# Down-weight sums of a two-FFN encoder layer, queued pair by pair behind a store of the gate and up stage

## The chip, the cores and the metric

One core of a Trainium2 chip runs the whole layer as one program. The metric is the device time of one execution, in microseconds; lower is better. Engines are named as the profile does: PE (TensorE matmuls), PEld (its weight loads), DVE (VectorE), ACT (ScalarE), POOL (GpSimd), SP (SyncE, which here issues most loads).

## The reference

One layer of a hybrid encoder on x of shape (1, 1024, 1024) in float32: an FFN, a mixing sub-layer (attention and a two-way recurrent scan) and a second FFN, each between RMS norms. The change touches the FFNs alone:

```python
def _swiglu(h, w_gate, w_up, w_down):
    return (jax.nn.silu(h @ w_gate) * (h @ w_up)) @ w_down

f = _swiglu(_rmsnorm(h, ffn1_pre_g), ffn1_w_gate, ffn1_w_up, ffn1_w_down)
h = h + 0.5 * _rmsnorm(f, ffn1_post_g)
# ... mixing sub-layer ...
f = _swiglu(_rmsnorm(h, ffn2_pre_g), ffn2_w_gate, ffn2_w_up, ffn2_w_down)
h = h + 0.5 * _rmsnorm(f, ffn2_post_g)
```

w_gate and w_up are 1024 x 2816, w_down is 2816 x 1024.

## The kernel before

Every float32 product is made of three passes: an operand is split into a rounded high part and the rest (`halves`, `split`: ACT makes the high part on L185, DVE the rest on L186), and PE adds high x high, high x low and low x high.

Both matrix products of an FFN are made by a fast scheme of seven products of half-size blocks in place of eight. In the **gate and up stage** the two matrices are the two block rows; one step j treats a column of 128 features. There are 22 columns. For each j, four weight blocks raw (two of the gate, two of the up weights, 256 KB each) are loaded by SP (L283) into a ring of eight buffers, DVE combines them (`left`, L60 to L63; L60 is the first and reads both up blocks), seven products of 12 matmuls run on PE (`multiply`, L81, numbered 1, 2, 6, 7, 5, 3, 4 in that order) into PSUM tiles gu, and DVE and ACT gather them (`gather`, L86 and after). A split weight is in a ring of eight (wh, wl).

When product 3 or 4 of a column has been gathered, `store` multiplies the two results on DVE (L114) and keeps a tile. Two columns make a *pair* m; its four tiles are the blocks of the left operand of the **down stage**. From them POOL forms the differences and sums that the seven down products need (L117, L126) and stores all seven to DRAM (`put`, L116, tensor d_hid). The tile that ends the pair's first column is called a11; its call of `store` sends it off with `put(1, ...)`, and then a21 minus it with `put(7, ...)`.

The right operand of the down stage also needs sums of blocks, here of w_down, which depend on no activation. `down_sums(m)` makes them: SP loads four blocks of w_down (L181 by way of `load`) into four tiles ws0 to ws3, POOL makes four differences in place (L145) and stores each to DRAM (L146, tensor d_ws). Each of the four tags has one buffer, so a pair's loads must wait until the stores of the pair before have left it. The down stage reads d_ws first in its third product.

The order on each engine is not written by hand. A scheduler takes the traced instructions, with the data and buffer dependences between them, and lists them per engine by priority and readiness; every engine and every DMA queue then works through its list in order. An instruction that depends on nothing but weights may so be listed far ahead of where the code writes it.

Of the kernel before, what the change touches and what calls it, by code (L numbers as in the profile page):

```python
# [36 lines left out]
class _GateUp:  # L37
# [72 lines left out]
    def store(self, j, half, x):  # L110


        G, H = self.K.nc.gpsimd, self.H
        self.K.nc.vector.tensor_tensor(x[:, 0], x[:, 0], x[:, 1], op=OP.mult)  # L114
        H[j % 2, half] = x
        put = lambda n, y: G.dma_start(self.hid[n - 1, j // 2], y)  # L116
        sub = lambda o, a, b: G.tensor_tensor(o, a, b, op=OP.subtract)  # L117
        if (j % 2, half) == (0, 0):
            a11, a21 = H[0, 0], H[0, 1]
            put(1, a11[:, 0])  # L120
            sub(a21[:, 1], a11[:, 0], a21[:, 0])
            put(7, a21[:, 1])
        elif (j % 2, half) == (1, 1):
            a11, a21, a22 = H[0, 0], H[0, 1], H[1, 1]
            put(4, a22[:, 0])
            G.tensor_tensor(a22[:, 1], a21[:, 0], a22[:, 0], op=OP.add)  # L126
            put(5, a22[:, 1])
            sub(a11[:, 1], a22[:, 1], a11[:, 0])
            put(6, a11[:, 1])
        elif (j % 2, half) == (1, 0):  # L130
            a11, a12 = H[0, 0], H[1, 0]
            put(2, a12[:, 0])
            sub(a12[:, 1], a12[:, 0], a11[:, 1])
            put(3, a12[:, 1])
            H.clear()
# [16 lines left out]
    def rest(self, f, psum):  # L152
        for j in range(NJ):
            for n in (1, 2, 6, 7, 5, 3, 4):
                if (n, j) not in self.done:
                    self.multiply(n, j, f, psum)
                if (n, j) in self.P:
                    self.gather(n, j)
            if j % 2 == 0:
                self.down_sums(j // 2)  # L160


class _Kernel:
# [84 lines left out]
    def post(self, p, ft, t, gb, scale, res, store):  # L248

        nc = self.nc  # L250
        rows = slice(t * 128, (t + 1) * 128)
        r = p.tile([128, D], F32, name="res", tag="res")
        self.load(r, res[rows, :])
        rs = self.inv_rms(p, ft, scale)
        nc.vector.scalar_tensor_tensor(ft, ft, rs, gb, op0=OP.mult, op1=OP.mult)  # L255
        nc.vector.tensor_tensor(ft, ft, r, op=OP.add)  # L256
        self.nc.sync.dma_start(store[rows, :], ft)
# [9 lines left out]
    def hand_over(self, p, psum, f, i, order, gb, scale, res, store, gcol, x, ready=lambda half: None):  # L267

        self.post(p, f[order[i]], order[i], gb, scale, res, store)
        for j in ([i - 1] if i % 4 else []) + ([i] if i % 4 == 3 else []):  # L270
            if i == j == NT - 1:
                ready(0)
            self.pre(p, f[order[j]])
            if j % 4 == 3:
                self.feature_major(psum, [f[t] for t in order[j - 3:j + 1]], gcol, x, 0, j // 4)
        if i == NT - 1:
            ready(1)
# [1155 lines left out]
```

## Time and profile before

| | |
|---|---|
| median of 3 runs | 2482.37 us (2478.59 to 2485.76) |
| profiled execution | 2491.72 us, span 2489.9 us |
| PE busy | 2255.0 us (91%) |
| DVE busy | 1708.7 us (69%) |
| ACT busy | 1041.1 us (42%) |
| POOL busy | 575.1 us (23%) |
| mean granted PE clock | 0.933 |
| L145, sums of down weights on POOL | 88, 118.2 us |
| ws loads, d_ws stores | 88 and 88, 256.0 KB each |

The first FFN's gate and up stage runs from the start to about 510 us of the span, the second's from about 1800 to 2260 us. Busy times overlap between engines. A row such as "A <- B: t, n, x" in the views of waits says that A's engine stood idle for t us in n pieces, the longest of x us, and that B ended that. Numbers are microseconds from the span's start; a view of windows gives the busy time of each engine in each stretch.

### The profile page before, as it was taken

The page shows a single profiled execution, that of the slowest core. Times are in us where ns is not written, and L with a number is a line of the kernel's source. Part 1 is how long each engine was busy: PE and PEld are TensorE (multiplying, and loading weights), DVE is VectorE, ACT ScalarE, POOL GpSimd, SP SyncE. Part 2 cuts the span into 40 slices and gives each one's busy share as a digit, 9 for nine tenths or more (in the row PEclk, how much of TensorE's full clock was granted, in tenths as well). Part 3 has the DMA queues.
Part 4 walks back from the last instruction along what each step waited for, and adds up shares of the span by engine and source line. Part 5 has one row for each costly group of instructions (what it writes and reads, how often), then busy time and mean ns, then how long its engine had stood idle before and what let it go on. Part 6 is the DMA issues. An engine that isn't in the chain of part 4 may idle for free. (4 is left out here: it accounts for less than half of the span.)

```text
span 2489.9 us, 39287 instructions
## 1 busy us (share of the span) xinstructions
PE 2255.0 (91%) x14532; PEld 1818.7 (73%) x14532; DVE 1708.7 (69%) x2917; ACT 1041.1 (42%) x1918; POOL 575.1 (23%) x668
## 2 busy tenths in 40 slices
PE   5869999999999998999987698888778899999997
PEld 4657888878877676778766576765556788887886
DVE  8768877765676345666566767725896987876565
ACT  4313333354577403656445354444431233335452
POOL 7772221210000010111101211122368422221000
PEclk8889999999999998999996688888889899999999
DMA  5773333376662414322366766467567433336655
GB/s 149 232 228 110 110 106 98 110 242 193 196 223 93 185 43 151 85 76 72 99 172 170 174 160 171 118 198 234 169 204 252 156 107 102 105 107 234 195 188 182
DMA packets 359763, 386.03 MB, mean 155 GB/s; under 512 B 73618, under 2 KB 268050, under 8 KB 359572
## 3 DMA queue, kind: packets, MB, share of 16 engines
q1 hardware_dynamic: 314272, 289.02, 38.6%
q0 software_dynamic: 27248, 86.05, 9.4%
q10 hardware_dynamic: 18052, 8.46, 1.3%
q8 instruction: 114, 1.87, 0.3%
q14 instruction: 77, 0.63, 0.1%
HBM read 257.53 MB, written 125.89 MB: 154 GB/s over the span
## 5 line engine op out<-in xcount | busy, mean ns | idle before, releaser
L81 PE MATMUL gu<-xh,wh 128*128 128x512 f32 x704 | 282.1, 401 | 47.3 <-DVE row L86 44.1
L185 ACT ACTIVATE wh<-raw 128x512 fp32r<-128x512 f32 (+1 forms) x273 | 169.5, 630 | 367.9 <-PE gu L81 261.1
L86 DVE TENSOR_TENSOR row<-gu,row 128x512 f32<-128x512 f32 x308 | 207.0, 684 | 122.8 <-PE gu L81 122.1
L81 PE MATMUL gu<-xl,wh 128*128 128x512 f32 x704 | 279.5, 397 | 0.0
L81 PE MATMUL gu<-xh,wl 128*128 128x512 f32 x704 | 278.8, 396 | 0.6 <-DVE wl L186 0.6
L186 DVE TENSOR_TENSOR wl<-raw,wh 128x512 fp32r<-128x512 f32 (+1 forms) x273 | 260.1, 955 | 4.8 <-ACT wh L185 4.1
L414 PE MATMUL pd<-gl,gwh 128*128 128x512 f32 x616 | 240.4, 390 | 2.5 <-DVE gl L186 2.5
L414 PE MATMUL pd<-gh,gwh 128*128 128x512 f32 x616 | 239.5, 390 | 0.6 <-DVE row L86 0.6
L414 PE MATMUL pd<-gh,gwl 128*128 128x512 f32 x616 | 239.7, 389 | 0.0
L186 DVE TENSOR_TENSOR gwl<-graw,gwh 128x512 fp32r<-128x512 f32 (+1 forms) x176 | 110.5, 631 | 129.4 <-ACT gwh L185 127.5
L116 POOL DMA_DIRECT2D d_hid<-row x154 | 84.7, 551 | 489.6 <-DVE row L114 470.3
L81 PEld LDWEIGHTS gu<-xh,wh 128*128 128x128 f32 x704 | 136.1, 193 | 78.8 <-DVE row L86 46.4
L185 ACT ACTIVATE gwh<-graw 128x512 fp32r<-128x512 f32 (+1 forms) x176 | 101.4, 576 | 193.4 <-PE pd L414 162.2
L81 PEld LDWEIGHTS gu<-xh,wl 128*128 128x128 f32 x704 | 135.2, 192 | 29.3 <-DVE wl L186 0.8
L81 PEld LDWEIGHTS gu<-xl,wh 128*128 128x128 f32 x704 | 135.7, 193 | 28.3
L414 PEld LDWEIGHTS pd<-gl,gwh 128*128 128x128 f32 x616 | 115.6, 188 | 27.8 <-DVE gl L186 4.2
L414 PEld LDWEIGHTS pd<-gh,gwh 128*128 128x128 f32 x616 | 115.6, 188 | 25.3 <-DVE row L86 1.0
L414 PEld LDWEIGHTS pd<-gh,gwl 128*128 128x128 f32 x616 | 115.7, 188 | 24.0
L145 POOL TENSOR_TENSOR ws<-ws 128x512 f32<-128x512 f32 x88 | 118.2, 1343 | 46.6 <-DMA ws<-in_ffn_w_down_dram 45.6
L186 DVE TENSOR_TENSOR gl<-raw,gh 128x512 fp32r<-128x512 f32 x160 | 112.2, 713 | 16.4 <-ACT gh L185 16.0
L185 ACT ACTIVATE gh<-raw 128x512 fp32r<-128x512 f32 x160 | 98.0, 620 | 29.2 <-DMA raw<-in_ffn_w_down_dram 20.1
L114 DVE TENSOR_TENSOR row<-row 128x512 f32<-128x512 f32 x88 | 95.7, 1089 | 3.7
(354 smaller groups left out, 5248.1 us busy)
## 6 DMA issues: line engine op xcount, KB each, us to landing
d_hid<-row POOLq DMA_DIRECT2D x154, 256.0 KB, 2.5
graw<-d_hid SPq DMA_DIRECT2D x132, 256.0 KB, 3.1
raw<-in_ffn_w_gate_dram SPq DMA_DIRECT2D x88, 256.0 KB, 3.1
raw<-in_ffn_w_up_dram SPq DMA_DIRECT2D x88, 256.0 KB, 2.9
ws<-in_ffn_w_down_dram SPq DMA_DIRECT2D x88, 256.0 KB, 3.5
d_ws<-ws POOLq DMA_DIRECT2D x88, 256.0 KB, 2.8
raw<-d_ws SPq DMA_DIRECT2D x88, 256.0 KB, 2.7
raw<-in_ffn_w_down_dram SPq DMA_DIRECT2D x66, 256.0 KB, 3.3
```

What stands on the lines that cost most here:

```text
L81: self.K.nc.tensor.matmul(ps, a[:, k, :], b[:, k, :], start=(k == 0 and i == 0), stop=(k == 3 and i == 2))
L86: add = lambda o, x: V.tensor_tensor(o, ps, x, op=OP.add)
L114: self.K.nc.vector.tensor_tensor(x[:, 0], x[:, 0], x[:, 1], op=OP.mult)
L116: put = lambda n, y: G.dma_start(self.hid[n - 1, j // 2], y)
L145: G.tensor_tensor(o, a, b, op=OP.subtract)
L185: self.nc.scalar.activation(h, src, AF.Copy)
L186: (eng or self.nc.vector).tensor_tensor(l, src, h, op=OP.subtract)
L414: T.matmul(ps[x], a[:, ts], b, start=(m == 0 and k == 0), stop=(m == NM - 1 and k == 2))
```

## The change

`down_sums` is traced in a block that gives every POOL instruction in it (the four differences and the four stores) an edge to `begun`, the POOL instruction that stores the pair's own a11. The edge fixes the order of issue on POOL alone; nothing waits for that store to end. The loads of ws on SP get no edge of their own; the scheduler places them anew, since the buffers they fill come free at other times.

```diff
@@ store
         if (j % 2, half) == (0, 0):
             a11, a21 = H[0, 0], H[0, 1]
-            put(1, a11[:, 0])
+            self.begun = put(1, a11[:, 0])
             sub(a21[:, 1], a11[:, 0], a21[:, 0])
             put(7, a21[:, 1])
@@ rest
             if j % 2 == 0:
-                self.down_sums(j // 2)
+                with self.K.tc.issue_after(self.begun.ins):
+                    self.down_sums(j // 2)
```

The changed file is one line longer, so lines from L160 on count one higher in it.

On POOL, first FFN, the place of the first stores of gate and up tiles (d_hid0). Tiles carry numbers here: row_613 is a11 of pair 0, row_612 and row_617 are its a21 and a22, and ws_2284 to ws_2287 are the down-weight tiles of pair 5. Before:

```order
L145 TENSOR_TENSOR ws_2285<-ws_2287,ws_2285 128x512
L146 DMA d_ws0_92<-ws_2285 128x512
L145 TENSOR_TENSOR ws_2287<-ws_2287,ws_2284 128x512
L146 DMA d_ws0_92<-ws_2287 128x512
L116 DMA d_hid0_86<-row_613 128x512
L117 TENSOR_TENSOR row_612<-row_613,row_612 128x512
L116 DMA d_hid0_86<-row_617 128x512
L116 DMA d_hid0_86<-row_612 128x512
L126 TENSOR_TENSOR row_617<-row_612,row_617 128x512
L116 DMA d_hid0_86<-row_618 128x512
L116 DMA d_hid0_86<-row_617 128x512
L117 TENSOR_TENSOR row_613<-row_617,row_613 128x512
```

Ahead of these rows stand the 20 sums of pairs 0 to 4 and the first of pair 5. Now (ws_794 to ws_797 are those of pair 0):

```order
L342 TENSOR_TENSOR row_220<-row_220,row_224 128x512
L343 TENSOR_TENSOR row_224<-row_224,row_220 128x512
L116 DMA d_hid0_86<-row_617 128x512
L116 DMA d_hid0_86<-row_613 128x512
L117 TENSOR_TENSOR row_612<-row_613,row_612 128x512
L145 TENSOR_TENSOR ws_794<-ws_795,ws_794 128x512
L116 DMA d_hid0_86<-row_612 128x512
L146 DMA d_ws0_92<-ws_794 128x512
L145 TENSOR_TENSOR ws_795<-ws_797,ws_795 128x512
L126 TENSOR_TENSOR row_617<-row_612,row_617 128x512
L146 DMA d_ws0_92<-ws_795 128x512
L145 TENSOR_TENSOR ws_797<-ws_797,ws_794 128x512
```

The sums of pair 0 now come behind the store of row_613 and between the other stores of that pair, and no sum of another pair is ahead of them; each later pair's four stand in the same way behind its own a11.

On SP, first FFN, the loads of the weights of block column 4 (gate: raw_1178 and raw_1200, up: raw_1221 and raw_1223), among loads of down weights. Before (ws_1965 to ws_1968 belong to pair 4, ws_2284 to ws_2287 to pair 5, ws_2603 and ws_2604 to pair 6):

```order
L181 DMA ws_1965<-in_ffn1_w_down_dram 128x512
L181 DMA ws_1966<-in_ffn1_w_down_dram 128x512
L181 DMA ws_1968<-in_ffn1_w_down_dram 128x512
L181 DMA ws_1967<-in_ffn1_w_down_dram 128x512
L181 DMA ws_2284<-in_ffn1_w_down_dram 128x512
L181 DMA ws_2285<-in_ffn1_w_down_dram 128x512
L181 DMA ws_2287<-in_ffn1_w_down_dram 128x512
L181 DMA ws_2286<-in_ffn1_w_down_dram 128x512
L283 DMA raw_1221<-in_ffn1_w_up_dram 128x4x128
L181 DMA ws_2603<-in_ffn1_w_down_dram 128x512
L181 DMA ws_2604<-in_ffn1_w_down_dram 128x512
L283 DMA raw_1223<-in_ffn1_w_up_dram 128x4x128
```

Now (raw_1067 and raw_1069 are up blocks of column 3, raw_1343 to raw_1386 blocks of column 5, ws_1008 to ws_1011 belong to pair 1):

```order
L284 DMA raw_1067<-in_ffn1_w_up_dram 128x4x128
L284 DMA raw_1069<-in_ffn1_w_up_dram 128x4x128
L284 DMA raw_1178<-in_ffn1_w_gate_dram 128x4x128
L284 DMA raw_1200<-in_ffn1_w_gate_dram 128x4x128
L284 DMA raw_1221<-in_ffn1_w_up_dram 128x4x128
L284 DMA raw_1223<-in_ffn1_w_up_dram 128x4x128
L182 DMA ws_1008<-in_ffn1_w_down_dram 128x512
L182 DMA ws_1009<-in_ffn1_w_down_dram 128x512
L284 DMA raw_1343<-in_ffn1_w_gate_dram 128x4x128
L182 DMA ws_1011<-in_ffn1_w_down_dram 128x512
L284 DMA raw_1365<-in_ffn1_w_gate_dram 128x4x128
L182 DMA ws_1010<-in_ffn1_w_down_dram 128x512
```

Before, 22 ws loads of pairs 1 to 6 and the four of pair 0 stand ahead of the last up block of column 4 (raw_1223). Now only pair 0's four do, and pair 1's come after it. The second FFN changes in the same way, and there the last pair's four ws loads and sums stand where the down stage's first loads begin, as in the first.

## The prediction

> **What bounds the kernel now.** I read the page first, then the stages by windows, then what each engine waited for in the two that were not full, and last the order of the two queues there.
>
> ```profile
> span 2489.9 us, 39287 instructions
> PE gu L81 13%; PE pd L414 8%; POOL ws L145 1%; PE po L1063 1%; DMA ws<-in_ffn_w_down_dram 1%; DMA raw<-in_ffn_w_up_dram 1%; DMA f_y<-d_y 1%; DVE wl L186 1%; DMA d_ws<-ws 1%; DVE row L255 0%; DVE row L256 0%; DMA d_y<-yb 0%; PE st L936 0%; PE var L1003 0%; DVE row L265 0%
> L86 DVE TENSOR_TENSOR row<-gu,row 128x512 f32<-128x512 f32 x308 | 207.0, 684 | 122.8 <-PE gu L81 122.1
> L186 DVE TENSOR_TENSOR wl<-raw,wh 128x512 fp32r<-128x512 f32 (+1 forms) x273 | 260.1, 955 | 4.8 <-ACT wh L185 4.1
> d_ws<-ws POOLq DMA_DIRECT2D x88, 256.0 KB, 2.8
> ```
>
> PE's gate and up matmuls are the largest piece of the chain that ended last (13%), and the sums' own line (ws L145) and their DMAs stand on that chain with 1% each, which is odd for work that nothing needs before the down stage. The next view takes four stretches of the two gate and up stages; its columns are the window, its length, busy time (with count) of PE, PEld, DVE, ACT and POOL, the granted clock, the DMA share and GB/s.
>
> ```profile
> 100.00:200.00 100.00, 74.18 (x304) 60.00 (x303) 74.38 (x73) 20.01 (x36) 70.85 (x80) 0.86 0.65 215
> 225.00:500.00 275.00, 275.00 (x1215) 227.72 (x1214) 216.32 (x287) 88.37 (x145) 64.11 (x79) 1.00 0.32 103
> 1850.00:1950.00 100.00, 80.72 (x337) 64.98 (x336) 76.66 (x80) 21.87 (x39) 75.51 (x83) 0.90 0.69 233
> 1950.00:1975.00 25.00, 25.00 (x112) 20.68 (x111) 24.88 (x28) 7.17 (x13) 11.88 (x15) 1.00 0.39 141
> ```
>
> From 225 to 500 us PE is busy all the time at clock 1.00: 1215 rows in 275 us, 0.2263 us a matmul. That is the pace of the stage. From 100 to 200 us the same stage passes only 304 rows at a mean clock of 0.86, and in the second FFN 337 rows in 100 us at 0.90. The time is lost early in each FFN, not spread over it. The gaps of PE there (start, length, instruction, idle time before it and its releaser):
>
> ```profile
> 129.10 0.79 PE L81 MATMUL gu<-xh,wh 128*128 128x512 f32 x1 [6.11 <-DVE row L86]
> 152.38 0.50 PE L81 MATMUL gu<-xh,wh 128*128 128x512 f32 x1 [1.82 <-DVE row L86]
> 189.61 0.80 PE L81 MATMUL gu<-xh,wh 128*128 128x512 f32 x1 [17.89 <-DVE row L86]
> ...
> 1901.45 0.54 PE L81 MATMUL gu<-xh,wh 128*128 128x512 f32 x1 [2.66 <-DVE row L86]
> 1937.99 0.79 PE L81 MATMUL gu<-xh,wh 128*128 128x512 f32 x1 [15.61 <-DVE row L86]
> ```
>
> 25.8 us of gaps in the first FFN, 18.3 us in the second, all ended by the DVE addition that empties a bank of gu (L86). DVE itself was starved, not busy. Its waits in the two FFNs, then SyncE's queue between 60 and 200 us (columns: us in total, times, longest):
>
> ```profile
> DVE s L60 <- DMA raw<-in_ffn_w_up_dram: 26.0, 4, 14.8
> DVE s L60 <- DMA raw<-in_ffn_w_up_dram: 24.0, 5, 13.4
> SPq L181 <- DMA d_ws<-ws: 65.0, 31, 5.6
> SPq L181 <- POOL ws L145: 22.7, 9, 5.4
> ```
>
> DVE's in-order queue stood for 26.0 and 24.0 us behind the first addition of a block column's combinations (L60), which wants two blocks of the up weights. SyncE's queue, which issues those loads in order, stood for 65.0 + 22.7 us behind loads of down weights (L181) whose tile ws was not yet free. The longest wait, row by row:
>
> ```profile
> 160.04 0.38 SPq L283 DMA_DIRECT2D raw<-in_ffn_w_gate_dram  x1
> 164.44 6.88 SPq L181 DMA_DIRECT2D ws<-in_ffn_w_down_dram  x3
> 171.41 0.39 SPq L283 DMA_DIRECT2D raw<-in_ffn_w_up_dram  x1
> 171.89 3.88 SPq L181 DMA_DIRECT2D ws<-in_ffn_w_down_dram  x2
> 175.85 0.40 SPq L283 DMA_DIRECT2D raw<-in_ffn_w_up_dram  x1
> 180.61 1.71 DVE L60 TENSOR_TENSOR s<-raw 128x512 f32<-128x512 f32 x1 [14.81 <-DMA raw<-in_ffn_w_up_dram]
> ```
>
> The two up loads went out at 171.41 and 175.85, each behind ws loads, and DVE, idle for 14.81 us, could go on only at 180.61; PE stood until 189.61. The chain that ended last says the same of the second FFN (start, length, what):
>
> ```profile
> 1919.66 3.98 DMA d_ws<-ws
> 1924.43 4.23 DMA raw<-in_ffn_w_up_dram
> 1930.64 2.39 DVE wl L186
> ```
>
> A store of one sum, then the up load that stood behind the next ws load, then DVE. So the loop sum, store, load of the next pair's ws sets the pace of SyncE's queue, and with it that of DVE and PE.
>
> **The change part by part.** No instruction is added or removed. What moves: 88 sums and 88 stores on POOL, and, by what the scheduler makes of it, the 88 ws loads on SyncE.
>
> (1) *The stalls in full flow.* Before, 22 ws loads of pairs 1 to 6 stood ahead of column 4's last up block; now none of them does (rows of the change above), and the loads for columns 2 to 4 go out as soon as their raw tiles are free. First FFN: 304 rows at 0.2263 us need 68.8 us, they took 100: 31.2 us lost, of which 25.8 are the gaps and 5.4 the slower clock after them. Second FFN: 337 rows need 76.3 us: 23.7 us lost. All of it goes if DVE can keep pace, together 54.9 us. It can: when it was starved it had already done everything that it had data for. What is late next is PE itself, as from 225 to 500 us.
>
> (2) *The start of each stage.* POOL's sums slow DVE: DVE reads of two SBUF tiles get long beside them. The rows below are the two starts, all engines, then POOL's sums and their stores alone (columns then: window, length, POOL busy, clock, DMA share, GB/s), and what PE waited for there.
>
> ```profile
> 40.00:67.50 27.50, 10.70 (x46) 8.72 (x47) 27.08 (x22) 8.47 (x16) 21.43 (x19) 0.69 0.39 127
> 1812.00:1848.00 36.00, 24.21 (x111) 18.69 (x111) 33.48 (x37) 15.66 (x27) 23.20 (x25) 0.89 0.60 199
> 40.00:67.50 27.50, 10.14 (x10) 0.69 0.39 127
> 1812.00:1848.00 36.00, 23.18 (x24) 0.89 0.60 199
> 67.17 1.94 PE L329 MATMUL pt<-ident,row 128*128 128x128 f32 x8 [6.45 <-DVE xl L186]
> 88.72 1.71 PE L329 MATMUL pt<-ident,row 128*128 128x128 f32 x8 [2.41 <-DVE t5l L186]
> 1844.16 1.97 PE L329 MATMUL pt<-ident,row 128*128 128x128 f32 x8 [7.12 <-DVE t5l L186]
> L186 DVE TENSOR_TENSOR wl<-raw,wh x21: 674/681/2395, 101.4 to 197.0; 128x512 fp32r<-128x512 f32 x21
> ```
>
> An undisturbed DVE row of this size takes about 0.68 us (the median of the last row). From 40 to 67.5 us DVE needed 27.08 us for 22 rows, 15.0 us undisturbed: 12.1 us lost beside 21.43 us of POOL, of which 10.14 are ws work. That share of the loss is 5.7 us, and PE waited for DVE there (6.45 us). The factor sums that PE's transposes need also stand earlier on POOL. From 1812 to 1848 us: 33.48 us for 37 rows, 25.2 undisturbed, 8.3 lost, and nearly all of POOL's 23.20 us is ws work; the 7.12 us wait for t5l stands in that stretch. I take 6 us for each start. Bounds: 0, if other work of DVE or POOL comes to bind in the same place, up to 10.1 us (all the ws work) and 8.3 us.
>
> (3) *The sums beside the steady stage.* Now every pair has its four sums and stores in a stretch that had none:
>
> ```profile
> L145 POOL TENSOR_TENSOR ws<-ws x88: 1257/1302/1847, 40.1 to 1951.3; 128x512 f32<-128x512 f32 x88
> 113.29 0.56 POOL L146 DMA_DIRECT2D d_ws<-ws  x1 [0.30 <-POOL ws L145]
> ```
>
> Four times 1.302 + 0.56 us is 7.4 us of POOL a pair, 81.9 us an FFN (44 of each); POOL has room (64.11 of 275 us busy). DVE pays: in 225 to 500 us 287 rows took 216.32 us, 21.2 more than 287 x 0.68, beside 64.11 us of POOL: 0.33 us lost for each us of POOL. In 100 to 200 us the same sum gives 74.38 - 73 x 0.68 = 24.7 over 70.85: 0.35. So DVE loses 27 us more an FFN. A stage is 154 products of 12 matmuls, 418 us at 0.2263; some 310 us of it follow 200 us, and at 58.7 idle us in 275 DVE has 66 us spare there. It fits, with DVE busy near 88%. The nearest row is 1950 to 1975 us: POOL busy 11.88 of 25, DVE 24.88, and PE passes 112 rows without a gap. I take 0 for PE; bounds 0 and 27 us an FFN, if every lost us of DVE reached PE.
>
> (4) *POOL's queue.* The stores of gate and up tiles no longer queue behind 23 sums. A pair's sums stand behind its first store; the next come a column later (84 matmuls, 19 us), so 7.4 us delay none. No gap of PE above waits for such a store, so I count 0.
>
> (5) *SyncE's queue.* A ws load still waits until its tile's last sum is stored: about 7.4 us of sums and 2.8 us of landing (the page's d_ws row) after the pair's first store, some 11 us into the next block column. Behind it in the queue stand blocks that DVE wants two columns later, because eight raw tiles hold two columns: a column's 84 matmuls, 19 us, or more of cover. I count 0; its failure is a rival below.
>
> (6) *The end of each stage.* The last pair's four ws loads now stand among the first loads of the down stage, and four sums run there. Four issues at about 0.4 us are 1.6 us on SyncE; I take 1.5 us of PE for each FFN, bounds 0 and 8 (all four sums with their stores).
>
> Sum: 31.2 + 23.7 + 6 + 6 - 3 = 63.9, say 64 us. The profiled execution took 1.8 us beyond its span of 2489.9, 2491.72 in all, which is 9.35 us over the median of the runs, 2482.37. I take the saving from the median, since none of its terms grows with what the profile adds: 2418 us.
>
> **A rule weighed.** The rows first: L186, which reads two SBUF tiles, ranges from 674 to 2395 ns around a median of 681, while L86, which reads PSUM and SBUF, keeps a mean of 684 beside the same POOL. The Trainium skill, "SBUF — State Buffer", section "Who interferes with whom", says that such a DVE instruction and a GpSimd instruction that reads SBUF exclude each other for the whole instruction, whoever comes first. The rows agree in kind. Taken to its end for term (3), each sum blocks DVE in full: 44 x 1.302 = 57.3 us of DVE an FFN instead of 27, against 66 us spare. By the rows the sum is 64 us; by the rule it stays so in the mean, but bursts could reach PE and leave 37 us or less; that is rival A.
>
> **The rivals.** A: *DVE becomes the bound.* The four sums come just when DVE has the next column's additions and splits in a row, all of two SBUF tiles. For it: the wide range of L186. Against: 1950 to 1975 us, and that DVE empties a bank only once in some 2.7 us of PE. Price: between half and all of 27 us an FFN, so 27 to 54 us back; 2482 - 64 + 27 = 2445 us, at worst 2472.
>
> B, slower: *SyncE's queue stalls once a pair instead of once at the start.* Place: a ws load of pair m waits for the stores of pair m - 1 just made, and the up loads stand behind it. A late up load costs what it cost before: a gap such as 6.11 us and 1.8 us of slow clock (5.4 us over three gaps), 7.9 us; over 20 pairs 158 us, 2482 - 64 + 158 = 2576. It decides once PE loses over 64 / 22 = 2.9 us a pair, which needs the 11 us wait to outlast 19 us of cover. For it: a shorter form of this very wait is the present loss. Against: now only one pair's sums stand in the way, and their inputs are there.
>
> C, no change: *the starvation has another cause*, such as DMA landing or DVE's own load, and comes back at the same place: 2482. Against: the up load landed in 4.23 us, while DVE waited up to 14.81 us, and PE runs full once the sums are over.
>
> **How the numbers follow.** Forecast 0.80, with its own range of 2409 to 2443 (terms 2 and 6 at their ends: 54.9 + 18.4, or 54.9 - 16); A 0.13; B 0.03; C 0.04. This kernel's runs differ by 7 us, 0.3%, which is about what a measurement can tell from no change. Faster by more than that: the forecast and nearly all of A, 0.93; within it 0.04; slower 0.03. Range: low 2482 - 54.9 - 10.1 - 8.3 = 2409, less 5 us for the spread of runs, 2404; high is A's 2445. Predicted 2418.
>
> **What would show it.** Right: no wait of L60 for up loads above 2 us in either FFN; SyncE's waits of L181 for d_ws without a DVE wait behind them; PE full from about 100 us and from about 1860 us; ws rows on POOL spread over both stages, with DVE there near 88%; the gaps of 17.89 and 15.61 us gone. Wrong: repeated PE gaps by L86 in the steady stage with DVE busy (A) or DVE idle for up loads (B), the three large gaps still there (C), or a new wait of several us where the down stage begins.

## The result and the profile after

The changed kernel takes 2418.94 us (median of 4 runs, 2416.97 to 2419.88) against 2484.07 us (2478.59 to 2498.82, 4 runs) before: a ratio of 0.973, with a 95% interval of 0.969 to 0.977. That is 65.1 us less. The profiled execution of before lay 7.65 us above its median and that of after (2416.97 us) 1.97 us below its own, so the two traces differ by 74.7 us where the medians differ by 65.1; gains below are read from the traces, stage by stage. In the three later series of runs the kernel before had medians of 2489.97, 2490.76 and 2491.95 us (7 runs each), and the changed kernel, run again beside the second, 2416.68 us: 74.1 us less. The saving is 65 to 74 us, then.

The page after, in the order of the lines shown of before (span, busy time of the engines, chain by line, two groups):

```profile
span 2415.2 us, 39328 instructions
PE 2244.4 (93%) x14532; PEld 1812.9 (75%) x14532; DVE 1780.8 (74%) x2917; ACT 1030.2 (43%) x1918; POOL 571.2 (24%) x668
PE gu L81 15%; PE pd L415 9%; PE po L1064 1%; DMA f_y<-d_y 1%; DVE wl L187 1%; DVE row L256 0%; PE st L937 0%; DVE row L86 0%; DVE row L257 0%; PE y L937 0%; DVE row L266 0%; ACT junk L244 0%; PE var L1004 0%; PE yc L995 0%; PE bonus L1011 0%
L86 DVE TENSOR_TENSOR row<-gu,row 128x512 f32<-128x512 f32 x308 | 206.9, 684 | 22.7 <-PE gu L81 22.1
L187 DVE TENSOR_TENSOR wl<-raw,wh 128x512 fp32r<-128x512 f32 (+1 forms) x273 | 277.3, 1019 | 6.0 <-ACT wh L186 5.1
```

The sums (ws), their stores and the late up loads have left the chain; PE's gate and up matmuls have grown from 13% to 15% of it. DVE is 72 us busier (1780.8 against 1708.7), though it has the same instructions: the idle time of L86 behind PE fell from 122.8 to 22.7 us, and the splits (L187) rose from 955 to 1019 ns.

Windows of after, then two of before for the same stretches (columns as in the prediction):

```profile
40.00:67.50 27.50, 16.69 (x80) 13.27 (x81) 25.45 (x30) 15.18 (x27) 13.97 (x9) 0.75 0.26 77
67.50:100.00 32.50, 29.89 (x146) 24.26 (x145) 26.61 (x36) 12.12 (x21) 7.32 (x9) 1.00 0.20 65
100.00:200.00 100.00, 100.00 (x443) 82.84 (x442) 98.96 (x105) 28.23 (x51) 47.80 (x57) 1.00 0.49 169
225.00:450.00 225.00, 225.00 (x994) 186.37 (x994) 218.17 (x238) 68.93 (x119) 98.11 (x114) 1.00 0.47 162
1850.00:1950.00 100.00, 100.00 (x443) 82.85 (x442) 97.68 (x112) 30.42 (x55) 43.26 (x51) 1.00 0.48 164
```

```profile
67.50:100.00 32.50, 29.44 (x132) 24.08 (x131) 25.06 (x34) 15.34 (x25) 21.54 (x23) 0.82 0.72 223
225.00:450.00 225.00, 225.00 (x994) 186.32 (x993) 178.89 (x237) 72.12 (x119) 54.39 (x66) 1.00 0.31 104
```

A row is one matmul of the trace. From 100 to 200 us PE passes 443 rows at clock 1.00 instead of 304 at 0.86, 139 rows or 31.4 us at 0.2263 us each. In the steady stage PE passes 994 rows both times, but DVE now needs 218.17 of the 225 us (97.0%) where it needed 178.89: the sums cost it nearly all that it had left.

What is left of PE's longer waits, from 40 us on in the first gate and up stage, from 1790 us on in the second, and at the start of each down stage (three of under 1 us between 50 and 81 us are left out):

```profile
47.23 1.97 PE L330 MATMUL pt<-ident,row 128*128 128x128 f32 x8 [10.42 <-DVE xl L187]
60.48 1.23 PE L330 MATMUL pt<-ident,row 128*128 128x128 f32 x8 [1.78 <-DVE xl L187]
78.20 1.25 PE L330 MATMUL pt<-ident,row 128*128 128x128 f32 x8 [1.93 <-DVE t5l L187]
476.25 0.50 PE L415 MATMUL pd<-gl,gwh 128*128 128x512 f32 x1 [1.48 <-DVE gl L187]
1794.20 1.25 PE L330 MATMUL pt<-ident,row 128*128 128x128 f32 x8 [1.71 <-DVE t5l L187]
2191.75 0.50 PE L415 MATMUL pd<-gl,gwh 128*128 128x512 f32 x1 [0.64 <-DVE gl L187]
```

For a bank of gu (L86) PE waits once in the two stages, 0.28 us at 1846.57. The first wait of this list was longer before, and the prediction did not show it:

```profile
49.52 1.97 PE L329 MATMUL pt<-ident,row 128*128 128x128 f32 x8 [14.03 <-DVE xl L186]
```

The waits in the first FFN, DVE's for up weights and SyncE's for a free ws tile, then DVE's for up weights in the second FFN (us in total, times, longest):

```profile
DVE s L60 <- DMA raw<-in_ffn_w_up_dram: 0.9, 4, 0.3
SPq L182 <- DMA d_ws<-ws: 5.4, 1, 5.4
SPq L182 <- POOL ws L145: 2.4, 1, 2.4
DVE s L60 <- DMA raw<-in_ffn_w_up_dram: 1.9, 3, 1.4
```

DVE's 26.0 us behind the up loads are 0.9 us now (24.0 are 1.9 in the second FFN), and SyncE's 65.0 + 22.7 us behind ws tiles are two waits, of 5.4 and 2.4 us. Landmarks in PE's timeline of before give the size by FFN, the start of each down stage (the same wait for gl) and a matmul between the FFNs, which in after starts at 1708.87:

```profile
518.30 0.50 PE L414 MATMUL pd<-gl,gwh 128*128 128x512 f32 x1 [1.48 <-DVE gl L186]
1747.87 0.56 PE L1063 MATMUL pw<-woh,xh 128*128 128x512 f32 x1 [2.19 <-DVE row L1094]
2266.32 0.50 PE L414 MATMUL pd<-gl,gwh 128*128 128x512 f32 x1 [0.64 <-DVE gl L186]
```

So the first FFN ends its gate and up stage 518.30 - 476.25 = 42.05 us earlier, 3 us are given back by 1708.87, and the second gains 518.45 - 482.88 = 35.6 us (2266.32 - 1747.87 against 2191.75 - 1708.87).

### The profile page after: what moved, and what is told of

Same layout as the page of the kernel before. It is cut to its first block, busy times and chain, and to the rows that moved or that the text cites. A ratio compares the mean times of both kernels' runs of the same rounds, so it can differ in the third digit from the quotient of the medians.

```text
span 2415.2 us, 39328 instructions
## 1 busy us (share of the span) xinstructions
PE 2244.4 (93%) x14532; PEld 1812.9 (75%) x14532; DVE 1780.8 (74%) x2917; ACT 1030.2 (43%) x1918; POOL 571.2 (24%) x668
## 5 line engine op out<-in xcount | busy, mean ns | idle before, releaser
L187 DVE TENSOR_TENSOR wl<-raw,wh 128x512 fp32r<-128x512 f32 (+1 forms) x273 | 277.3, 1019 | 6.0 <-ACT wh L186 5.1
L86 DVE TENSOR_TENSOR row<-gu,row 128x512 f32<-128x512 f32 x308 | 206.9, 684 | 22.7 <-PE gu L81 22.1
L187 DVE TENSOR_TENSOR gwl<-graw,gwh 128x512 fp32r<-128x512 f32 (+1 forms) x176 | 118.1, 674 | 128.1 <-ACT gwh L186 124.1
L187 DVE TENSOR_TENSOR gl<-raw,gh 128x512 fp32r<-128x512 f32 x160 | 112.4, 714 | 15.9 <-ACT gh L186 15.4
L94 ACT ACTIVATE row<-row 128x512 f32<-128x512 f32 x44 | 27.9, 633 | 225.2 <-DVE row L86 217.7
```

Source lines behind the costliest of these rows:

```text
L86: add = lambda o, x: V.tensor_tensor(o, ps, x, op=OP.add)
L94: A.activation(y[:, 0], y[:, 0], AF.Silu)
L187: (eng or self.nc.vector).tensor_tensor(l, src, h, op=OP.subtract)
```

## The experiments

Theory Q: the loss was SyncE's in-order queue. Loads of ws that waited for a tile held up loads, and with them DVE and PE. Rivals: the sums' own weight on DVE; and, for what the change now costs, how near the kernel comes to rival A (DVE full) and rival B (the queue again).

**The loads alone taken off SyncE.** The kernel before, with the sums where they were (early), but their loads issued from POOL's queue:

```diff
-            self.K.load(t[q], self.wd[...])
+            G.dma_start(t[q], self.wd[...])
```

> The kernel before (no edge, POOL's sums still hoisted ahead of the first stores), but the ws loads are issued from POOL's own queue instead of SyncE's. Theory Q (SyncE's queue, blocked by ws loads, starves DVE and so PE): L60's waits for up loads fall from 26 and 24 us to under 2 us each, the PE gaps of 6.11, 17.89 and 15.61 us go, and 54.9 us come back, the terms of full flow; the start terms stay lost: about 2484 - 55 = 2429 us, 2420 to 2440. Rival K (POOL's hoisted sums beside DVE are what holds PE, whatever queue the loads are on): the sums stand as early as before and POOL gets 88 issues more, so 2470 to 2500 us.

Measured: 2449.15 us (2441.36 to 2451.52), ratio 0.983 (0.979 to 0.986). Both theories missed the time. Its windows, then DVE's wait for up loads in the first FFN:

```profile
40.00:67.50 27.50, 11.96 (x47) 9.71 (x48) 26.91 (x22) 8.19 (x15) 22.68 (x23) 0.62 0.51 157
67.50:100.00 32.50, 25.18 (x104) 20.23 (x103) 21.97 (x25) 12.58 (x21) 22.63 (x28) 0.73 0.56 182
100.00:200.00 100.00, 98.86 (x438) 81.27 (x436) 97.34 (x98) 28.14 (x50) 75.15 (x94) 1.00 0.65 210
DVE s L60 <- DMA raw<-in_ffn_w_up_dram: 4.3, 3, 1.8
```

From 100 to 200 us it passes 438 rows, 134 more than before (30.3 us): the stalls in full flow were the queue, since nothing but the loads' queue was changed, POOL's early sums are still there, and DVE's 26.0 us behind up loads are 4.3. But the start did not get better: 47 rows from 40 to 67.5 us (46 before, 80 after) and 104 from 67.5 to 100 (132 before, 146 after). And from 225 to 450 us it passes 966 rows instead of 994, behind one wait of 3.42 us for L86 at 229.99 and a slower clock after it. That is 28 rows (6.3 us) lost in each of two places, and its first FFN gains only 30.3 - 6.3 - 6.3 = 18 us by rows; its down stage begins at 501.56, 16.7 us earlier than before. So there were two losses: the queue (loads), and the start, which moving the loads alone does not bring back. This kernel does not show by itself that the early sums slow the start, since its loads now wait for their buffers in POOL's queue (7.6 us behind d_ws up to 105 us); the kernel without sums, below, bears on that too.

**One FFN at a time.** The edge only where ws belongs to the first FFN, and only where it belongs to the second:

```diff
-                self.down_sums(j // 2)
+                with ExitStack() as x:
+                    if self.ws is self.K.ws_d[0]:      # [1] in the other kernel
+                        x.enter_context(self.K.tc.issue_after(self.begun.ins))
+                    self.down_sums(j // 2)
```

> The edge in the first FFN only. In the two profiles the end of the first gate and up stage moved by 42 us and the second stage by 36 us more (with 3 us lost between them). If the two are independent: a saving of 33 to 42 us, 2442 to 2451 us. If the cause sat in one of them alone: either about 2419 or about 2484 us.

> The edge in the second FFN only. Independent: a saving of 28 to 36 us, 2448 to 2456 us, and with the first FFN's alone it adds up to the whole 65 us. Otherwise as for the first FFN alone, 2419 or 2484 us.

Measured: 2453.08 us (2452.61 to 2454.05), ratio 0.985 (0.982 to 0.988), a saving of 36.9 us; and 2460.53 us (2446.05 to 2466.73), ratio 0.987 (0.981 to 0.992), a saving of 29.4 us. The two make 66.3 us, which is the whole change within the spread of its runs (65 to 74 us). In each, the untouched FFN keeps its stalls; PE's largest gap in the second FFN of the one, and in the first FFN of the other:

```profile
1898.51 0.80 PE L81 MATMUL gu<-xh,wh 128*128 128x512 f32 x1 [12.45 <-DVE row L86]
```

```profile
187.35 0.80 PE L81 MATMUL gu<-xh,wh 128*128 128x512 f32 x1 [15.05 <-DVE row L86]
```

**No sums at all.** The changed kernel without ws loads, sums and stores; the down stage loads plain blocks of w_down in their place, so this part of the product is left out.

```diff
-                with self.K.tc.issue_after(self.begun.ins):
-                    self.down_sums(j // 2)
+                pass
...
-                src = ws[n - 4, m]
+                src = wd[(2 * m + n % 2) * 128:(2 * m + n % 2 + 1) * 128, n // 6 * 512:n // 6 * 512 + 512]
```

> No sums of down weights at all: ws loads, POOL's differences and their stores are left out, and the down stage loads single blocks of w_down in their place. What the sums still cost after the change. Theory (PE is full in both stages, so DVE's time beside the sums is hidden): 0 to 6 us faster than the changed kernel, 2413 to 2420 us, with DVE's busy time down by 54 us (0.33 us for each us of ws work on POOL, as predicted) to 126 us (the 54 and the 72 that DVE grew by). Rival A (DVE is the bound after the change): more than 10 us faster, below 2409 us.

Measured: 2414.38 us (2408.89 to 2421.33), ratio 0.969 (0.966 to 0.973), within the spread of after. Moved work still runs, and PE pays nothing for it; DVE pays, by 130 us, a little more than the 54 to 126 expected. The page's busy times:

```profile
PE 2233.0 (93%) x14532; PEld 1804.2 (75%) x14532; DVE 1650.8 (68%) x2917; ACT 1044.9 (43%) x1918; POOL 412.2 (17%) x492
```

The windows of the start and of the steady stage:

```profile
40.00:67.50 27.50, 17.82 (x80) 14.05 (x81) 25.23 (x30) 14.85 (x27) 13.60 (x9) 0.72 0.26 77
67.50:100.00 32.50, 29.89 (x133) 24.28 (x132) 24.05 (x36) 12.03 (x21) 4.75 (x7) 0.89 0.16 49
225.00:450.00 225.00, 225.00 (x995) 186.29 (x994) 179.13 (x236) 72.69 (x119) 54.43 (x66) 1.00 0.31 105
```

With neither sums nor their loads the start passes 213 rows from 40 to 100 us, against 178 before and 226 after (from 67.5 us on PE is as busy as after, at a clock of 0.89 instead of 1.00). Moving the loads alone left it at 151. Together the two kernels put most of the start's loss on the early sums.

The 88 sums cost DVE 1780.8 - 1650.8 = 130 us, 1.48 us each, against 1708.7 - 1650.8 = 57.9 us, 0.66 us each, where they stood before. In the steady stage it is 218.17 - 179.13 = 39.0 us for 24 sums, 1.63 us each: more than the 1.30 us that a sum itself takes. The trace of after shows why, POOL first, then DVE:

```profile
267.47 1.30 POOL L117 TENSOR_TENSOR row<-row 128x512 f32<-128x512 f32 x1
268.73 1.30 POOL L145 TENSOR_TENSOR ws<-ws 128x512 f32<-128x512 f32 x1
271.06 1.30 POOL L145 TENSOR_TENSOR ws<-ws 128x512 f32<-128x512 f32 x1
273.24 1.30 POOL L145 TENSOR_TENSOR ws<-ws 128x512 f32<-128x512 f32 x1
275.42 1.30 POOL L145 TENSOR_TENSOR ws<-ws 128x512 f32<-128x512 f32 x1
...
267.25 3.33 DVE L60 TENSOR_TENSOR s<-raw 128x512 f32<-128x512 f32 x1
270.50 2.42 DVE L187 TENSOR_TENSOR wl<-raw,wh 128x512 fp32r<-128x512 f32 x1
272.85 2.26 DVE L61 TENSOR_TENSOR raw<-raw 128x512 f32<-128x512 f32 x1
275.02 2.25 DVE L63 TENSOR_TENSOR raw<-raw 128x512 f32<-128x512 f32 x1
277.20 0.68 DVE L86 TENSOR_TENSOR row<-gu,row 128x512 f32<-128x512 f32 x1
```

The pair's first store comes just ahead of DVE's four operations of two SBUF tiles in a row. Each of them ends some 0.55 us after a sum ends (270.58 after 270.03, 272.92 after 272.36), so DVE passes one per sum; the first, L60, stood beside two POOL operations in turn (L117 and a sum) and took 3.33 us. L86, which reads PSUM, takes its usual 0.68 us. From one sum's start to the next is 2.18 us (273.24 to 275.42: the sum, 0.30 us, the store of 0.56 us), and in that time DVE passes one operation that alone takes some 0.6: nearly 1.6 us lost for each sum.

The prediction cites the Trainium skill, "SBUF — State Buffer", section "Who interferes with whom", for an exclusion of the two, by whoever comes first. The trace agrees that they exclude each other: here no such DVE operation ends during a sum. It does not agree on the order: each of the four is recorded as starting before the sum that it ends behind (270.50 against 271.06 for L187). And the loss of a sum, 1.63 us, is more than the 1.30 us that the prediction took the rule to cost.

**Another place in the pair.** The sums behind the pair's last store, and one sum behind each of the four stores put(1), put(5), put(6), put(3), beside the changed kernel run again. Behind the last:

```diff
-            self.begun = put(1, a11[:, 0])
+            put(1, a11[:, 0])
...
-            put(3, a12[:, 1])
+            self.begun = put(3, a12[:, 1])
...
-            if j % 2 == 0:
+            if j % 2:
```

Spread:

```diff
-            self.begun = put(1, a11[:, 0])
+            self.begun = [put(1, a11[:, 0])]
...
+            self.begun.append(put(5, a22[:, 1]))       # and put(6, ...), put(3, ...)
...
-        for n, o, a, b in (...):
-            G.tensor_tensor(o, a, b, op=OP.subtract)
-            G.dma_start(self.ws[n - 4, m], o)
+        for (n, o, a, b), begun in zip((...), self.begun):
+            with self.K.tc.issue_after(begun.ins):
+                G.tensor_tensor(o, a, b, op=OP.subtract)
+                G.dma_start(self.ws[n - 4, m], o)
...
-            if j % 2 == 0:
-                with self.K.tc.issue_after(self.begun.ins):
-                    self.down_sums(j // 2)
+            if j % 2:
+                self.down_sums(j // 2)
```

> The changed kernel once more, on the chip of the three variants beside it, so that they can be compared with it there: 2419 us, 2410 to 2430, and a ratio of 0.973 to the kernel before.

> The pair's four sums stand behind its last store (the end of its second column) instead of behind a11 at the end of its first. If it matters only that sums come pair by pair, and DVE's lost time stays hidden: 2419 us within 5, PE full in both stages. Rival (the place of the burst matters, since here it follows the pair's three other POOL sums without a break and meets the same run of DVE instructions): PE gaps once a pair, 2430 us or more.

> The pair's four sums are parted, one each behind the stores put(1), put(5), put(6) and put(3). If DVE's higher loss after the change comes from four sums in one burst that meets a run of two-SBUF additions and splits (L60 to L63, L187), DVE's busy time falls by 20 us or more from 1780.8, with the time at 2419 within 5, since PE is full either way. If the loss comes from DVE being busy at nearly all times, so that each POOL sum always meets it: DVE's busy time stays within 20 us.

Measured: 2416.68 us (2414.29 to 2419.88) for the changed kernel, ratio 0.970 (0.967 to 0.974); 2416.66 us (2408.13 to 2420.89), 0.970 (0.966 to 0.974) behind the last store; 2416.05 us (2407.8 to 2420.96), 0.970 (0.966 to 0.973) spread. The time is the same, and DVE's busy time is not: 1780.0, 1727.0 and 1759.5 us. The window of the steady stage with the sums behind the last store:

```profile
225.00:450.00 225.00, 225.00 (x994) 186.45 (x993) 197.78 (x240) 69.97 (x119) 96.59 (x112) 1.00 0.47 160
```

DVE's wait for up weights there, in the first FFN:

```profile
DVE s L60 <- DMA raw<-in_ffn_w_up_dram: 17.0, 9, 3.6
```

The window of the steady stage with the sums spread:

```profile
225.00:450.00 225.00, 225.00 (x994) 186.43 (x994) 208.72 (x237) 69.24 (x120) 96.54 (x113) 1.00 0.47 158
```

A sum costs DVE 0.87 us behind the last store ((1727.0 - 1650.8) / 88), 1.24 us spread, 1.48 us behind the first. The fall behind the last store, 53.0 us, is clear; the one of the spread sums, 20.5 us, is barely past the 20 us that were to decide. What a GpSimd sum costs DVE hangs on its place, that is, by the rows above, on what DVE has queued at that moment. As long as PE is full, none of it is time. But the row of waits is a warning: behind the last store, DVE waits 17.0 us for up loads again (0.9 in after), hidden so far.

**More work on POOL, until something breaks.** One or three more additions behind each sum at the old place, and one more behind each sum at the pair's end; the sums come out two or eight times too large:

```diff
             G.tensor_tensor(o, a, b, op=OP.subtract)
+            G.tensor_tensor(o, o, o, op=OP.add)        # three of them in the second kernel
             G.dma_start(self.ws[n - 4, m], o)
```

> The changed kernel with one more POOL addition of the same size behind each of the 88 differences (the sums come out doubled), before it is stored. It asks how far DVE is from being the bound after the change, where it was busy 218.17 of 225 us from 225 to 450 us. By the rate measured since (the run without sums: 130 us of DVE for 163.5 us of ws work on POOL, 0.8): 44 x 1.3 us more of POOL is 46 us more of DVE an FFN, of which some 12 are spare: 34 us an FFN reach PE, about 2487 us, 2460 to 2500, with gaps of PE ended by L86 in the steady stage while DVE is busy. By the rate in the prediction (0.33, DVE near 88%): 19 us more of DVE, which fits, so at most 2425 us and no gaps.

> The changed kernel with three more GpSimd additions of the same size behind each of the 88 sums (the sums then come out eight times too large). The run with one more added 95 us of POOL, 34 us of DVE (0.36 us for each us of POOL) and 14 us of time, with DVE busy 222.83 of 225 us in the steady stage. Theory full: VectorE has no room left, so nearly all that further additions cost it reaches TensorE: three times 95 us of POOL at 0.36 are 103 us of VectorE, less the 20 us that fit before: 2500 us (2475 to 2530), with VectorE busy 99% in the steady stage and TensorE waiting for L86 over and over. Theory yield: a full VectorE gives the additions less and less (they wait, not it): three times 14 us, 2459 us (2440 to 2470).

> The four sums behind the last store of the pair (there DVE was busy 1727 us instead of 1780, at the same time of the run), with one more GpSimd addition behind each sum as in the run that took 14 us longer (the sums come out doubled). Theory place: what a sum costs VectorE hangs on what VectorE has to do just then, and at this place there is room: VectorE has 27 us to spare in 225 here, so one more addition a sum fits, 2417 to 2422 us, with VectorE under 95% in the steady stage. Theory total: only the total of GpSimd work counts, and the time is that of the run with one more at the old place, 2426 to 2436 us.

Measured: one more, 2430.38 us (2425.8 to 2436.24), ratio 0.976 (0.971 to 0.980); three more, 2552.87 us (2546.89 to 2553.19), ratio 1.025 (1.023 to 1.027); one more at the pair's end, 2465.77 us (2460.29 to 2469.3), ratio 0.991 (0.989 to 0.993). Every size given ahead was missed: the first lies between its two theories, the second above both, and the third above both, at the place that costs DVE least. Added lines shift the numbers: L183 and L285 below are L182 and L284 of after. The window of the steady stage with one more:

```profile
225.00:450.00 225.00, 224.82 (x985) 184.28 (x984) 222.83 (x237) 64.77 (x118) 120.25 (x134) 1.00 0.46 156
```

The same window with three more:

```profile
225.00:450.00 225.00, 203.20 (x858) 165.38 (x856) 222.64 (x203) 54.93 (x100) 154.65 (x163) 0.96 0.41 137
```

Two of PE's gaps there:

```profile
231.77 0.80 PE L81 MATMUL gu<-xh,wh 128*128 128x512 f32 x1 [2.84 <-DVE row L86]
275.83 0.79 PE L81 MATMUL gu<-xh,wh 128*128 128x512 f32 x1 [4.29 <-DVE row L86]
```

With one more addition DVE is busy 222.83 of 225 us and PE loses 9 rows. With three more DVE cannot do more (222.64 us) and does 203 instructions where it did 237; PE passes 858 rows and stands once a pair for L86, every 44 us (231.77, 275.83) where 168 matmuls take 38.0. That is rival A, reached. The two steps show the edge: the first 95 us of POOL work cost 14 us, since DVE still had some room; the next 197 us (862.4 against 665.0 us of POOL) cost 122.

One more at the pair's end breaks in another way. The window of its steady stage:

```profile
225.00:450.00 225.00, 216.46 (x938) 176.10 (x937) 189.92 (x219) 60.43 (x110) 124.44 (x132) 0.99 0.47 153
```

Its waits in the first FFN, DVE's and SyncE's:

```profile
DVE s L60 <- DMA raw<-in_ffn_w_up_dram: 55.0, 10, 6.9
SPq L183 <- DMA d_ws<-ws: 88.7, 40, 4.4
```

Its timeline at one pair, SyncE's rows and then DVE's:

```profile
238.04 5.94 SPq L183 DMA_DIRECT2D ws<-in_ffn_w_down_dram  x3
244.08 0.96 SPq L285 DMA_DIRECT2D raw<-in_ffn_w_up_dram  x2
249.90 0.69 DVE L60 TENSOR_TENSOR s<-raw 128x512 f32<-128x512 f32 x1 [6.88 <-DMA raw<-in_ffn_w_up_dram]
```

DVE has room (189.92 of 225 us) and PE loses 56 rows. Three ws loads hold SyncE's queue from 238.04 to 243.98 until sums are stored, the up loads go out at 244.08, and DVE stands for 6.88 us, once in most pairs. By these rows that is rival B: the stall of before, come back in small pieces, 88.7 us of SyncE's time behind d_ws where after has 5.4. So the place that is the kindest to DVE is the worse one for the queue, and the two limits bind at different places.

## Why the prediction was right

It forecast 2418 us (2404 to 2445) and 2418.94 was measured. Point by point:

- *What bounds it, and term (1).* Right in size: 31.2 us forecast, 139 rows or 31.4 us found from 100 to 200 us; from 1850 to 1950 us 443 rows against 337, 24.0 us for the 23.7. Shown to be the queue of loads by the kernel with only the loads moved (30.3 us back in the same window).
- *Term (2), the starts.* Under-sized. From 40 to 100 us PE passes 226 rows instead of 178, 10.9 us and not 6; in the second FFN 35.6 less the 24.0 leaves 11.6. Both are above the bounds that the term gave, 10.1 and 8.3. The step that failed is the share: I gave the sums' part of POOL's time (10.14 of 21.43) the same part of DVE's loss. PE's waits there for DVE fell from 14.03, 6.45 and 2.41 us to 10.42, 1.78 and 1.93; the longest of them, which ends in the stretch that the term prices, was not among its rows. The start stays slow with only the loads moved (151 rows) and is fast without sums (213), so the early sums account for most of it; which part came through DVE and which through the factor sums queued behind them on POOL was not separated.
- *Term (3), the sums beside the steady stage.* The conclusion (0 on PE) held, the size did not: 0.33 us of DVE for each us of POOL and 88% were forecast, 1.63 us a sum, or 0.87 for each us of its 1.86, and 97.0% were found. An average over a stage where POOL's work fell on mixed DVE work was carried to a place where it falls on four two-tile operations. At the pair's end the forecast share was met, 197.78 of 225 us, 88%, at a rate still above the forecast one: 0.87 us a sum over the run is 0.47 for each us of POOL. The clock, the matmul pace and the rows from 1850 to 1950 us show no loss, because 7 us in 225 were left. The rule weighed there, taken as one sum's length for each sum, would have given 57.3 us an FFN; 65 were found (130 / 2).
- *Terms (4) and (5), the queues.* 0 was right: no gap of PE by a late store, one wait of 5.4 us of SyncE for d_ws in each FFN. The cover of a column that term (5) named is real but not large: it was used up when the sums came later and took longer.
- *Term (6), the ends.* Over-sized: 1.5 us each forecast, 0 found; PE's waits at the down stage's start are the same 1.48 and 0.64 us.
- The errors of (2) and (6) act the same way, 11 us and 3 us more saving, which by the traces gives 77.7 us less the 3 us given back between the FFNs, the 74.7 found. The sum of 63.9 was made from a trace and is to be held against that 74.7: it was 11 us too small. That 2418 still met the median rests on the step that took the saving from the median of 2482.37 and not from the profiled execution; from its 2491.72 the sum would have given 2428. The median of 2482.37 lay some 8 us below those of the later series (2489.97 to 2491.95), and that made up for most of the 11 us: how near 2418 came is luck, though the way, the cause of the largest term and the range were right.
- *Rivals.* C is out. A and B did not happen, but the chances given them hid how near they were: one more addition a sum reaches A, and A or B is chosen by the place in the pair.

## What to carry to other kernels

Work that depends on nothing was not free early here: its loads hold an in-order queue while they wait for a buffer, so look at what is queued behind a load that can wait, and tie such work to the stage that has room for it. When it is tied to a point, read what the other engines do in the few microseconds behind that point; a mean rate from elsewhere in the trace was off by more than a factor of two here, while the time did not move. Then see how much room is left, since the next change on that engine may find none.

## What was not expected of the hardware

A GpSimd sum of 1.30 us, set among DVE operations that read two SBUF tiles, cost DVE 1.63 us in the mean of the steady stage, more than its own length: between sums and their stores DVE passed one operation in some 2.2 us instead of one in 0.6. And the loss is not linear in POOL's work: 95 us more of it cost 34 us of DVE and 14 us of time when DVE was 97% full, 292 us more cost 154 us of DVE and 136 us of time.
